# Five stages for all of a gated mixer's first product, with half of the modulation vector made in PE's column groups

## The chip, the cores and the metric

One Trainium2 chip, one of its cores. The metric is the device time of one execution in microseconds (us); a kernel's figure is the median of its runs. Before the change it is 2622.1 us (three runs, 2620.47 to 2630.4).

## What is computed

Three blocks on 256 rows of 2048 channels. The change lies in the first, and there in its entry:

```python
cond = silu(c)                               # one vector of 2048
mod = cond @ ada_w[i] + ada_b[i]             # 2048 x 6144
shift, scale, gate = split(mod, 3)
h = rms_norm(x, pre_g[i]) * (1 + scale) + shift
u, v, z = split(h @ w_in, 3)                 # 2048 x 12288
u = gelu(u); v = layer_norm(gelu(v), norm_g)
vm = einsum('gts,bnsgc->bntgc', w_s * mask, v) + b_s
y = (u * vm * silu(z)) @ w_out
x = x + gate * rms_norm(y, post_g[i])
```

All weights are float32 in HBM and are read once.

## The kernel before

Every weight matrix is loaded in chunks of 512 KB (two tiles of 128 rows by 512 columns) on SP's queue. A chunk ("piece") is split into a rounded part `wh` (ACT, line 239) and a remainder `wl` (DVE, line 242); PE multiplies three times for each tile of 128 rows (x high by wh, x high by wl, x low by wh: lines 301 to 303 with rows of x as stationary operand, 293 and 294 with weights as stationary operand). Six `raw` buffers hold loaded pieces, four pairs `wh`, `wl` hold split ones. `plan` writes the order of all loads into one list; `_issue` issues them in that order as buffers come free, `piece` hands split pieces to PE.

The first product is the v third of `h @ w_in`: eight groups of 512 columns, 16 tiles of 128 rows (k tiles) deep. It needs h, and h needs shift and scale of layer 0, that is 32 MB of `ada_w` before the last k tile. So the program goes in four stages of four k tiles each. `ada` loads scale and shift for the next 512 channels as eight chunks of 1 MB (rows of 512 columns) into a ring of five slots and multiplies them by `cond`: on DVE as one instruction for each 128 rows (lines 429 and 431), but for half of the scale's rows as a matmul with `cond` as a stationary operand of one column (line 427). Matmuls with ones (line 446) sum over the partitions and turn the row into a column, then `scale_done` and `h_tiles` (lines 569 to 574) make h. In each stage PE then takes v groups 3, 0, 1 and 2; groups 0 to 2 stay in six banks of PSUM over all stages, group 3 is summed in SBUF (lines 750 and 752, two banks). Groups 4 to 7 follow after the last stage as ordinary products (`gemm_tm`), and with them `spatial` loads and transposes `sgu_w_s` (lines 699 to 710), and `mix` puts 0.7 of a chunk of the remaining modulation (`rest`, 96 chunks of 512 KB: gate of layer 0, shift and scale of layer 1) beside each piece. Then come u (64 pieces) and z (64 pieces), with more of `rest`.

All engines work through their own instructions in the written order; waits are semaphores, so an instruction that waits holds up all behind it on its engine.

Of the kernel before, what the change touches and what calls it, by code (L numbers as in the profile page):

```python
# [16 lines left out]
P = 128  # L17
T = 256
# [53 lines left out]
class Kernel:  # L72
    def __init__(self, ctx, tc, ins, out):
# [4 lines left out]
        self.RAW, self.LOOK, self.AHEAD = 6, 3, 3  # L78
        self.g = ctx.enter_context(tc.tile_pool(name="g", bufs=1))
# [376 lines left out]
    def plan(self):  # L456
# [3 lines left out]
        self.h_done = [0] * 4  # L460
        for s in range(4):
            ring = [7, 8, 9, 10, 11]
            a = self.ada(0, 0, s, None, kt=4, ring=ring)
            b = self.ada(0, 1, s, (lambda s=s: self.h_stage(s)), kt=4, pe=2, ring=ring)
            if s == 0:
                for e in (b[0], a[0], b[1]):
                    e.ring = [1, 2, 3]
            E += [b[0], a[0], b[1], a[1], b[2], a[2], a[3], b[3]]
# [10 lines left out]
        for g in range(4, 8):  # L479
            main += self.group(("v", g), w_in, 4096 + g * 512, 16)  # L480
# [6 lines left out]
        E += self.mix(main, rest, [(40, 0.7), (64, 0.42), (64, 0.2), (56, 0.6)])  # L487
# [88 lines left out]
    def h_stage(self, s):  # L576
        self.scale_done(0, s)
        for j in range(4 * s, 4 * s + 4, 2):
            self.h_tiles(0, (j, j + 1), self.R0)
            self.split_ahead(2)  # L580


    def setup(self):
# [16 lines left out]
        nc.scalar.activation(out=self.cond, in_=ps[:, 0:16], func=AF.Silu)  # L600
        rows = self.slot(6).rearrange("p (a n) -> p a n", n=P)
# [8 lines left out]
        for tt in range(2):  # L610
            self._issue()
            nc.sync.dma_start(out=xt[tt], in_=i["x"][0, tt * P:tt * P + P, :])
        for _ in range(3):
            self._issue()
# [7 lines left out]
        self.wst = self.t("wst", [P, 16, P], pool=self.p0)  # L622
        self.bs = self.t("bs", [P, 16, P], pool=self.p0)
# [14 lines left out]
        self.prep_next()  # L638
        self.prep_next()
# [3 lines left out]
        for q in range(8):  # L643
# [6 lines left out]
            if q == 3:  # L650
                self.prep_next()
                self.prep_next()
# [8 lines left out]
        self.prep_next()  # L661
# [8 lines left out]
        self.start_stage()  # L670

    def start_stage(self):

        for _ in range(9):
            self.prep_next()

    def spatial(self, slot):
# [3 lines left out]
        ws = self.slot(slot).rearrange("p (g s) -> p g s", s=P)  # L681
        nc.sync.dma_start(out=ws, in_=i["sgu_w_s"][0].rearrange("g t s -> t g s"))
        nc.sync.dma_start(out=self.bs.rearrange("p g t -> p (g t)"), in_=i["sgu_b_s"].rearrange("o g t -> o (g t)").to_broadcast([P, 2048]))
        rows = self.slot(10)[:, 0:P]
        nc.vector.memset(rows[0:32, :], 0.0)
# [13 lines left out]
        nc.tensor.transpose(ps[:, 0:32], rows[0:32, :], self.identt[0:32, 0:32])  # L699
        yield  # L700
        nc.scalar.copy(self.cols[:, 2, 0:32], ps[:, 0:32])
        for q in range(4):
            ps = self.bank(5)
            for g in range(4):
                nc.tensor.transpose(ps[:, g * P:g * P + P], ws[:, q * 4 + g, :], self.identt)
# [7 lines left out]
    def sgu(self):  # L713
# [6 lines left out]
        def v_out(g):  # L720
            def evac(tt, ps):
                if uv[g] is None:
                    uv[g] = self.slot(4 + g).rearrange("p (i u t) -> p i u t", u=2, t=T)
                nc.scalar.activation(out=uv[g][:, :, 0, tt * P:tt * P + P], in_=ps.rearrange("p (i c) -> p i c", c=P), func=AF.Gelu, accum_out=stat[:, tt, g:g + 1])
            return evac

        banks = {(g, tt): self.bank(2 * g + tt) for g in range(3) for tt in range(2)}
        part = self.t("y4", [P, 4, T], pool=self.p0).rearrange("p (t i) n -> p t (i n)", t=2)
        self.banks([], [6])
        for s in range(4):  # L730
            self.split_ahead(2)
            for use in self.uses:
                if use:
                    use()
            self.uses = []
            for tt in range(2):
                banks[3, tt] = self.bank(6 + tt)
            for n in range(8):
                g = (3, 0, 1, 2)[n // 2]
                e, k0, kn, parts = self.piece(hold=s < 3)  # L740
                assert e.key == ("v", g)
                for tt in range(2):
                    ps = banks[g, tt]
                    for kk in range(kn):
                        k = n % 2 * 2 + kk
                        kt = s * 4 + k
                        self.mm_tm(ps, slice(0, 512), parts, kk, h(kt), tt, (k if g == 3 else kt) == 0, k == 3 if g == 3 else kt == 15)
                    if g == 3 and n % 2:
                        if s == 0:
                            nc.scalar.copy(part[:, tt, :], ps)  # L750
                        else:
                            nc.vector.tensor_tensor(out=part[:, tt, :], in0=part[:, tt, :], in1=ps, op=ALU.add)
                    if s == 3 and n % 2:
                        v_out(g)(tt, part[:, tt, :] if g == 3 else ps)
# [879 lines left out]
```

## Time and profile before

| | |
|---|---|
| median of three runs | 2622.1 us |
| the profiled execution | 2624.94 us, its span 2623.0 us |
| granted clock of TensorE, mean | 0.990 |
| busy PE, DVE, ACT | 98%, 71%, 53% of the span |
| read from HBM | 541.48 MB |

How to read it: PE is TensorE's matmul, PEld its load of the stationary operand, which runs beside PE. Busy time of PE is modelled, with overlapping records: the time that a matmul takes in a stream is the distance of starts. "Idle before" is how long the engine stood still before an instruction, with the releaser behind the arrow. Times within the program count from the start of the span. A float32 matmul that is not split leaves two records.

### The profile page before, as it was taken

What the parts mean: (1) busy time and instruction counts of PE and PEld (TensorE: products, weight loads), DVE (VectorE), ACT (ScalarE), POOL (GpSimd) and SP (SyncE); (2) the same over time, 40 slices, a digit from 0 to 9 for tenths busy, and PEclk for the clock granted to TensorE, in tenths of its full rate; (3) what the DMA queues carried; (4) which work ended last, traced back from release to release, by engine and by line L of the source; (5) the groups of instructions that cost most, each with busy time, mean ns of one, the idle gap of its engine ahead of it and who ended that gap; (6) DMA issues with size and microseconds to landing.
All of it is one profiled execution on the core that took longest, in us unless ns stands there. A gap on an engine that the chain in (4) does not pass through costs nothing. (4 is left out here: it accounts for less than half of the span.)

```text
span 2623.0 us, 36858 instructions
## 1 busy us (share of the span) xinstructions
PE 2558.0 (98%) x13884; PEld 2169.7 (83%) x13884; DVE 1852.5 (71%) x2700; ACT 1385.1 (53%) x2101; POOL 0.2 (0%) x4
## 2 busy tenths in 40 slices
PE   7999999999998999998999999999999999999999
PEld 4577888888886888887888888888888888888887
DVE  6877877777776778766778677668665555666665
ACT  3243644545454655556556666555544545555554
POOL 0000000000000000000000000000000000000000
PEclk8999999999998999999999999999999999999999
DMA  9989888666884677644545444555556666565664
GB/s 365 353 278 313 275 273 263 209 210 215 293 273 152 182 227 220 204 157 153 159 137 170 152 149 150 193 193 193 193 178 192 187 191 187 185 198 192 192 194 128
DMA packets 298524, 546.00 MB, mean 208 GB/s; under 512 B 27370, under 2 KB 40426, under 8 KB 297962
## 3 DMA queue, kind: packets, MB, share of 16 engines
q1 hardware_dynamic: 296618, 542.71, 64.2%
q8 instruction: 108, 1.77, 0.3%
q10 hardware_dynamic: 1728, 0.94, 0.1%
q14 instruction: 70, 0.57, 0.1%
HBM read 541.48 MB, written 2.10 MB: 207 GB/s over the span
## 5 line engine op out<-in xcount | busy, mean ns | idle before, releaser
L293 PE MATMUL b<-s,wh 128*128 128x512 f32 x4800 | 1696.8, 397 | 5.9 <-DVE s L941 4.6
L239 ACT CAST wh<-raw 128x1024 fp32r<-128x1024 f32 (+2 forms) x840 | 866.2, 1039 | 984.0 <-PE b L293 615.1
L294 PE MATMUL b<-s,wl 128*128 128x256 f32 x4800 | 1345.6, 280 | 0.5 <-DVE wl L242 0.5
L242 DVE TENSOR_TENSOR wl<-raw,wh 128x1024 fp32r<-128x1024 f32 (+2 forms) x840 | 1002.8, 1211 | 298.8 <-ACT wh L239 294.4
L293 PEld LDWEIGHTS b<-s,wh 128*128 128x128 f32 x4800 | 905.7, 189 | 208.4 <-issue 8.1
L294 PEld LDWEIGHTS b<-s,wl 128*128 128x128 f32 x4800 | 905.8, 189 | 1.6 <-DVE wl L242 0.8
L301 PE MATMUL b<-wh,s 128*128 128x512 f32 x816 | 329.3, 403 | 7.1 <-ACT s L570 6.1
L303 PE MATMUL b<-wh,s 128*128 128x512 f32 x816 | 323.7, 397 | 0.0
L302 PE MATMUL b<-wl,s 128*128 128x512 f32 x816 | 322.2, 395 | 1.3 <-DVE wl L242 1.3
L301 PEld LDWEIGHTS b<-wh,s 128*128 128x128 f32 x816 | 154.4, 189 | 51.2 <-ACT s L570 6.4
L314 DVE TENSOR_TENSOR cb<-b,ca 128x256 f32<-128x256 f32 x258 | 108.5, 422 | 115.0 <-ACT ca L308 110.9
L369 DVE TENSOR_TENSOR s<-s,s 128x1024 fp32r<-128x1024 f32 (+1 forms) x82 | 91.6, 1121 | 135.9 <-ACT s L368 135.9
L303 PEld LDWEIGHTS b<-wh,s 128*128 128x128 f32 x816 | 154.1, 189 | 39.6 <-DVE s L574 0.4
L302 PEld LDWEIGHTS b<-wl,s 128*128 128x128 f32 x816 | 154.5, 189 | 38.1 <-DVE wl L242 2.1
L431 DVE SCALAR_TENSOR_TENSOR ada<-raw,cond,ada 128x512 f32<-128x512 f32 x240 | 179.5, 748 | 3.5
L308 ACT COPY ca<-b 128x256 f32<-128x256 f32 x338 | 122.7, 366 | 45.5 <-PE b L294 34.1
L368 ACT CAST s<-s 128x1024 fp32r<-128x1024 f32 (+1 forms) x82 | 78.8, 961 | 12.7 <-DVE s L1010 6.6
L431 DVE SCALAR_TENSOR_TENSOR ada<-s,cond,ada 128x512 f32<-128x512 f32 x88 | 65.4, 751 | 7.8 <-DMA s<-in_ada_w 5.4
L314 DVE TENSOR_TENSOR s<-b,ca 128x256 f32<-128x256 f32 x72 | 29.9, 420 | 24.6 <-ACT ca L308 24.4
L293 PE MATMUL b<-yat,wh 128*128 128x512 f32 x128 | 44.4, 392 | 0.0
L427 PE MATMUL b<-s,cond 128*1 128x512 f32 x64 | 34.1, 660 | 8.4 <-DMA s<-in_ada_w 8.4
L1582 ACT ACTIVATE s<-s 128x256 f32<-128x256 f32 x64 | 26.8, 419 | 17.3 <-DVE s L1581 15.1
(305 smaller groups left out, 1451.5 us busy)
## 6 DMA issues: line engine op xcount, KB each, us to landing
raw<-in_sgu_w_in SPq DMA_DIRECT2D x192, 512.0 KB
raw<-in_w_in SPq DMA_DIRECT2D x148, 512.0 KB
raw<-in_ada_w SPq DMA_DIRECT2D x128, 512.0 KB
raw<-in_w_up SPq DMA_DIRECT2D x128, 512.0 KB
raw<-in_w_down SPq DMA_DIRECT2D x128, 512.0 KB
s<-in_ada_w SPq DMA_DIRECT2D x32, 1024.0 KB
raw<-in_sgu_w_out SPq DMA_DIRECT2D x64, 512.0 KB
raw<-in_mla_w_in SPq DMA_DIRECT2D x40, 512.0 KB
```

The costliest lines, as they stand in the source:

```text
L239: self.nc.scalar.copy(h, v[:, k0:k0 + kn, :])
L242: self.nc.vector.tensor_tensor(out=l, in0=v[:, k0:k0 + kn, :], in1=h.bitcast(F32), op=ALU.subtract)
L293: mm(ps[:, 0:512], h[:, kk, wsl], x, start=start, stop=False, skip_group_check=True)
L294: mm(ps[:, 0:256], l[:, kk, wsl], x[:, 0:256], start=False, stop=stop, skip_group_check=True)
L301: mm(ps, x[:, a:a + P], h[:, kk, wsl], start=start, stop=False, skip_group_check=True)
L302: mm(ps, x[:, a:a + P], l[:, kk, wsl], start=False, stop=False, skip_group_check=True)
L303: mm(ps, x[:, 256 + a:256 + a + P], h[:, kk, wsl], start=False, stop=stop, skip_group_check=True)
L308: self.nc.scalar.copy(c, ps[:, 256:512])
L314: self.nc.vector.tensor_tensor(out=o, in0=ps[:, 0:256], in1=c, op=ALU.add)
L368: self.nc.scalar.copy(dst[:, :, 0:256], raw)
L369: self.nc.vector.tensor_tensor(out=dst[:, :, 256:512], in0=raw, in1=dst[:, :, 0:256].bitcast(F32), op=ALU.subtract)
L431: nc.vector.scalar_tensor_tensor(out=acc[0], in0=v[:, k - k0, :], scalar=col, in1=acc[0], op0=ALU.mult, op1=ALU.add)
```

## The change

All eight v groups are now made in the stages, of which there are five, with 2, 2, 4, 4 and 4 k tiles. Groups 6 and 7 stay in four banks of PSUM; the other six share three banks in turn and are summed in SBUF after each stage (line 945, ACT copies, in the first; line 947, DVE adds, in the others), in the slots that later hold u and v, in `y4` and in `wst`. The whole of the scale goes to PE as float32 matmuls with a stationary operand of 32 columns (`condz`: `cond` in column 0, the rest zeros), each k tile of four in another group of 32 columns of the array (line 891, `tile_position`); an ACT copy (line 897) takes the four rows back. The whole of the shift goes to DVE (lines 875 and 877). Loads for the first two stages have rows of 256 columns, eight k tiles to a chunk. `walk` is the one list of pieces, modulation chunks and finishing steps from which all engines' instructions are written. `spatial` moves into u, and `rest` is mixed 0.75 to a piece of u and 0.24 to a piece of z, where it was 0.7 (v groups 4 to 7 and part of u), 0.42 and 0.2.

```diff
+        self.STAGES, self.ORDER, self.STAY = [0, 2, 4, 8, 12, 16], (0, 1, 6, 2, 3, 7, 4, 5), (6, 7)
...
-            a = self.ada(0, 0, s, None, kt=4, ring=ring)
-            b = self.ada(0, 1, s, (lambda s=s: self.h_stage(s)), kt=4, pe=2, ring=ring)
...
-            for g in (3, 0, 1, 2):
-                for k in range(2):
-                    E.append(self.chunk(("v", g), w_in, s * 512 + k * 256, 4096 + g * 512))
+            k0, k1 = self.STAGES[s + 1:s + 3]
+            n = (k1 - k0) * P
+            kt = 2048 // n
+            for r in range(0, 16, kt):
+                for part in range(2):
+                    e = self.chunk(None, i["ada_w"][0], r * P, part * 2048 + k0 * P, kt, n)
...
+            room = max(1, len(pieces) - 3)
...
+            put("rows", s=s + 1)
+            for kind, e, at in pieces[room:room + 1]:
+                put(kind, e, **at)
+            put("fin", s=s + 1)
+            for kind, e, at in pieces[room + 1:]:
+                put(kind, e, **at)
...
-        for g in range(4, 8):
-            main += self.group(("v", g), w_in, 4096 + g * 512, 16)
...
-        E += self.mix(main, rest, [(40, 0.7), (64, 0.42), (64, 0.2), (56, 0.6)])
+        E += self.mix(main, rest, [(64, 0.75), (64, 0.24), (56, 0.6)])
...
+        def mod(at):
...
+                q = slice(k % 4 * 32, k % 4 * 32 + 32)
+                nc.tensor.matmul(st["rows"][q, 0:n], self.condz[:, kt, :], v[:, k, :], start=kt < 4, stop=kt >= 12, tile_position=(0, k % 4 * 32), skip_group_check=True)
...
+        def product(at):
...
+                    if stay:
+                        b = self.STAY.index(g) * 2 + tt
+                    else:
+                        b = 4 + st["turn"] % 3
+                        st["turn"] += 1
...
+                if not stay:
+                    to = parts[g, tt]
+                    if s == 0:
+                        nc.scalar.copy(to, four(ps))
+                    else:
+                        nc.vector.tensor_tensor(out=to, in0=to, in1=four(ps), op=ALU.add)
...
+            if kind == "w" or kind == "mod":
+                ahead(4 if kind == "w" else 3)
```

How the order moves at three places. In the names `raw` is a loaded piece, `wh` and `wl` its two parts, `ada` a modulation sum, `b4` to `b6` the shared banks, `s7` to `s11` the ring of modulation chunks; the last number is a serial number.

DVE in the second stage before: one sum outside PSUM for the stage, behind the third split.

```order
L574 SCALAR_TENSOR_TENSOR s1_56_237<-cb_120_509,mod0_7_74,s1_56_237 128x256
L574 SCALAR_TENSOR_TENSOR s1_56_237<-cb_121_512,mod0_7_74,s1_56_237 128x256
L242 TENSOR_TENSOR wl_125_521<-raw_101_385,wh_112_480 128x1024
L242 TENSOR_TENSOR wl_131_533<-raw_105_409,wh_124_519 128x1024
L242 TENSOR_TENSOR wl_133_549<-raw_106_411,wh_130_531 128x1024
L752 TENSOR_TENSOR y4_67_248<-y4_67_248,b6_122_517 128x512
L752 TENSOR_TENSOR y4_67_248<-y4_67_248,b7_123_518 128x512
L242 TENSOR_TENSOR wl_135_567<-raw_107_413,wh_132_547 128x1024
L429 TENSOR_SCALAR ada_137_584<-s10_110_451,cond_8_75 128x512
```

DVE in the second stage now, from the split of the stage's first piece to the first sum.

```order
L859 TENSOR_TENSOR wl_114_464<-raw_78_291,wh_113_462 128x1024
L875 TENSOR_SCALAR ada_115_466<-s10_67_252,cond_8_75 128x512
L877 SCALAR_TENSOR_TENSOR ada_115_466<-s10_67_252,cond_8_75,ada_115_466 128x512 x3
L859 TENSOR_TENSOR wl_119_477<-raw_81_297,wh_118_475 128x1024
L877 SCALAR_TENSOR_TENSOR ada_115_466<-s7_82_307,cond_8_75,ada_115_466 128x512 x4
L859 TENSOR_TENSOR wl_125_505<-raw_87_329,wh_124_503 128x1024
L877 SCALAR_TENSOR_TENSOR ada_115_466<-s9_105_426,cond_8_75,ada_115_466 128x512 x4
L859 TENSOR_TENSOR wl_132_535<-raw_94_362,wh_131_533 128x1024
L947 TENSOR_TENSOR s4_51_195<-s4_51_195,b4_134_539 128x4x128
L947 TENSOR_TENSOR s4_51_195<-s4_51_195,b5_135_547 128x4x128
```

Between the first split and the first sum stand three further splits and three chunks of shift; the sum of bank b4_134 comes behind all of them.

PE at the same place now: the scale's four matmuls, and the second piece's product.

```order
L891 MATMUL b7_136_555<-s11_75_285,bs_11_82 32x512 x4
L303 MATMUL b6_142_574<-wh_118_475,s0_45_189 128x512
L304 MATMUL b6_142_574<-wl_119_477,s0_45_189 128x512
L305 MATMUL b6_142_574<-wh_118_475,s0_45_189 128x512
L303 MATMUL b6_142_574<-wh_118_475,s0_45_189 128x512
L304 MATMUL b6_142_574<-wl_119_477,s0_45_189 128x512
L305 MATMUL b6_142_574<-wh_118_475,s0_45_189 128x512
L303 MATMUL b4_143_582<-wh_118_475,s0_45_189 128x512
L304 MATMUL b4_143_582<-wl_119_477,s0_45_189 128x512
```

The second half of this piece goes into b4_143, which is the bank of b4_134.

DVE at the change to the third stage now, behind the first sums over partitions.

```order
L605 SCALAR_TENSOR_TENSOR s1_46_190<-cb_162_696,mod0_7_74,s1_46_190 128x256
L605 SCALAR_TENSOR_TENSOR s1_46_190<-cb_163_699,mod0_7_74,s1_46_190 128x256
L859 TENSOR_TENSOR wl_165_706<-raw_128_515,wh_164_704 128x1024
L600 SCALAR_TENSOR_TENSOR cb_167_710<-x_13_87,a10_26_117,R_42_181 128x256
L600 SCALAR_TENSOR_TENSOR cb_168_713<-x_13_87,a10_26_117,R_42_181 128x256
L605 SCALAR_TENSOR_TENSOR s1_46_190<-cb_167_710,mod0_7_74,s1_46_190 128x256
L605 SCALAR_TENSOR_TENSOR s1_46_190<-cb_168_713,mod0_7_74,s1_46_190 128x256
L875 TENSOR_SCALAR ada_169_718<-s8_137_560,cond_8_75 128x512
L877 SCALAR_TENSOR_TENSOR ada_169_718<-s8_137_560,cond_8_75,ada_169_718 128x512 x3
L859 TENSOR_TENSOR wl_171_725<-raw_133_537,wh_170_723 128x1024
L947 TENSOR_TENSOR wst_55_199<-wst_55_199,b6_174_731 128x512
L947 TENSOR_TENSOR wst_55_199<-wst_55_199,b4_175_739 128x512
```

The sum of bank b6_174, the bank that the last piece of the stage before (b6_180) takes for its second half, stands behind four instructions of h, a chunk of shift and two splits.

## Rows read from the trace of the kernel before

**Rows 1.** The page, part 1 (busy us) and the granted clock of part 2.
```profile
PE 2558.0 (98%) x13884; PEld 2169.7 (83%) x13884; DVE 1852.5 (71%) x2700; ACT 1385.1 (53%) x2101; POOL 0.2 (0%) x4
...
PEclk8999999999998999999999999999999999999999
```

**Rows 2.** Windows: busy us and (instructions) of PE, PEld, DVE, ACT, POOL; clock; DMA share; GB/s.
```profile
40.00:75.80 35.80, 33.74 (x129) 21.65 (x129) 31.04 (x46) 11.64 (x16) 0.00 (x0) 0.95 1.02 370
...
149.00:266.90 117.90, 114.94 (x507) 92.19 (x507) 84.87 (x95) 54.94 (x77) 0.00 (x0) 1.00 0.89 300
266.90:449.80 182.90, 182.90 (x1068) 161.42 (x1067) 135.44 (x180) 103.13 (x166) 0.00 (x0) 1.00 0.82 268
```

**Rows 3.** Timeline 0 to 48 us: start, duration, engine, line, idle before and releaser.
```profile
9.57 1.91 ACT L641 ACTIVATE x<-s 128x2048 f32<-128x2048 f32 x1 [5.87 <-DMA s<-in_x]
...
31.96 3.57 PE L427 MATMUL b<-s,cond 128*1 128x512 f32 x4 [4.73 <-DMA s<-in_ada_w]
...
35.46 3.57 PE L446 MATMUL b<-ones,ada 128*128 128x1 f32 x16
...
39.07 0.16 DVE L448 TENSOR_TENSOR mod<-b,cols 128x4 f32<-128x4 f32 x1 [1.55 <-PE b L446]
...
40.55 0.80 PE L301 MATMUL b<-wh,s 128*128 128x512 f32 x1 [1.51 <-ACT s L570]
```

**Rows 4.** Timeline of PE, 44 to 76 us.
```profile
44.10 0.40 PE L301 MATMUL b<-wh,s 128*128 128x512 f32 x1
...
46.20 0.40 PE L301 MATMUL b<-wh,s 128*128 128x512 f32 x1
...
50.49 1.88 PE L427 MATMUL b<-s,cond 128*1 128x512 f32 x4
...
72.32 1.95 PE L446 MATMUL b<-ones,ada 128*128 128x1 f32 x16
```

**Rows 5.** Groups of DVE by form, 40 to 76 us: count, busy us, mean ns, idle before.
```profile
L431 DVE SCALAR_TENSOR_TENSOR ada<-s,cond,ada 128x512 f32<-128x512 f32 x22 | 16.3, 751 | 1.0 <-DMA s<-in_ada_w 0.4
L242 DVE TENSOR_TENSOR wl<-raw,wh 128x1024 fp32r<-128x1024 f32 x8 | 9.5, 1217 | 0.4 <-ACT wh L239 0.4
...
L569 DVE SCALAR_TENSOR_TENSOR cb<-x,a,R 128x256 f32<-128x256 f32 x5 | 2.2, 481 | 0.0
L429 DVE TENSOR_SCALAR ada<-s,cond 128x512 f32<-128x512 f32 x2 | 1.0, 479 | 0.0
```

**Rows 6.** The same, 76 to 112 us: the sum outside PSUM.
```profile
L752 DVE TENSOR_TENSOR y<-y,b 128x512 f32<-128x512 f32 x2 | 1.4, 686 | 0.1
```

**Rows 7.** DMA, 90 to 98 us: packets, MB, share of 16 engines.
```profile
q1 hardware_dynamic: 1573, 3.09, 105.1%
```

**Rows 8.** DMA, 1276 to 1284 us, rows of 2 KB, queue not full.
```profile
q1 hardware_dynamic: 1054, 2.04, 77.7%
```

**Rows 9.** DMA, 1244 to 1252 us, nearly all rows of 1 KB, queue not full.
```profile
DMA packets 1083, 1.10 MB, mean 137 GB/s; under 512 B 33, under 2 KB 1059, under 8 KB 1083
...
q1 hardware_dynamic: 1083, 1.10, 48.6%
```

**Rows 10.** Instructions of line 427: ns min/median/max, first and last start.
```profile
L427 PE MATMUL b<-s,cond x64: 590/592/1061, 7.2 to 142.1; 128*1 128x512 f32 x64
```

**Rows 11.** Instructions of line 301, 200 to 300 us.
```profile
L301 PE MATMUL b<-wh,s x85: 392/392/501, 200.1 to 266.4; 128*128 128x512 f32 x85
```

**Rows 12.** Timeline of PE, 195 to 262 us: two of its waits.
```profile
216.96 0.50 PE L301 MATMUL b<-wh,s 128*128 128x512 f32 x1 [1.06 <-ACT wh L239]
...
225.17 0.66 PE L705 MATMUL b<-ident,s 128*128 128x128 f32 x4 [1.13 <-ACT cols L701]
```

**Rows 13.** Groups of DVE by form, 266.9 to 449.8 us (u).
```profile
L242 DVE TENSOR_TENSOR wl<-raw,wh 128x1024 fp32r<-128x1024 f32 x64 | 77.8, 1222 | 24.6 <-ACT wh L239 23.6
L431 DVE SCALAR_TENSOR_TENSOR ada<-raw,cond,ada 128x512 f32<-128x512 f32 x54 | 40.4, 748 | 0.7
L314 DVE TENSOR_TENSOR cb<-b,ca 128x256 f32<-128x256 f32 x32 | 13.2, 422 | 15.6 <-ACT ca L308 15.2
```

More of the change, by code (lines that the diff above doesn't have):

```diff
@@ new lines, in put @@
+        def put(kind, e=None, **at):
+            if e:
+                at["n"] = len(E)
+                E.append(e)
+            self.walk.append((kind, at))
+        for s in range(-1, len(self.STAGES) - 1):
+            pieces = []
+            if s >= 0:
+                k0, k1 = self.STAGES[s:s + 2]
+                for g in self.ORDER:
+                    for k in range(k0, k1, 2):
+                        pieces.append(("w", self.chunk(("v", g), w_in, k * P, 4096 + g * 512), dict(s=s, g=g, k=k)))
+            if s + 2 == len(self.STAGES):
+                for kind, e, at in pieces:
+                    put(kind, e, **at)
+                break
+            k0, k1 = self.STAGES[s + 1:s + 3]
+            n = (k1 - k0) * P
+            kt = 2048 // n
+            mods = []
+            for r in range(0, 16, kt):
+                for part in range(2):
+                    e = self.chunk(None, i["ada_w"][0], r * P, part * 2048 + k0 * P, kt, n)
+                    e.kind, e.ring = "ada0", [7, 8, 9, 10, 11]
+                    mods.append(("mod", e, dict(s=s + 1, part=part, r=r, kt=kt)))
+            done = 0
+            room = max(1, len(pieces) - 3)
+            for q in range(room if pieces else 0):
+                put(*pieces[q][:2], **pieces[q][2])
+                while done < len(mods) and (done + 0.5) * room < (q + 1) * len(mods):
+                    put(*mods[done][:2], **mods[done][2])
+                    done += 1
+            for kind, e, at in mods[done:]:
+                put(kind, e, **at)
+            put("rows", s=s + 1)
+            for kind, e, at in pieces[room:room + 1]:
+                put(kind, e, **at)
+            put("fin", s=s + 1)
+            for kind, e, at in pieces[room + 1:]:
+                put(kind, e, **at)
@@ L610, in setup @@
         for tt in range(2):
-            self._issue()
             nc.sync.dma_start(out=xt[tt], in_=i["x"][0, tt * P:tt * P + P, :])
-        for _ in range(3):
+        for _ in range(2):
             self._issue()
@@ L669, in setup, with spatial @@
         columns(1)
[L670 to L677, printed above, removed]
+    def spatial(self):
         nc, i = self.nc, self.i
         yield from self.idle(40)
[L681 to L682 removed]
+        self.wst = self.t("wst", [P, 16, P], pool=self.p0)
+        self.bs = self.t("bs", [P, 16, P], pool=self.p0)
+        nc.sync.dma_start(out=self.wst, in_=i["sgu_w_s"][0].rearrange("g t s -> t g s"))
         nc.sync.dma_start(out=self.bs.rearrange("p g t -> p (g t)"), in_=i["sgu_b_s"].rearrange("o g t -> o (g t)").to_broadcast([P, 2048]))
[L684 to L685 removed]
+        rows = self.t("rows", [32, P], pool=self.p0)
+        nc.vector.memset(rows, 0.0)
         rp = lambda ap: ap.rearrange("(b p) -> b p", p=P)
@@ L698, in spatial @@
         ps = self.bank(5)
[L699 removed]
+        nc.tensor.transpose(ps[:, 0:32], rows, self.identt[0:32, 0:32])
         yield
@@ L723, in evac @@
                     uv[g] = self.slot(4 + g).rearrange("p (i u t) -> p i u t", u=2, t=T)
-                nc.scalar.activation(out=uv[g][:, :, 0, tt * P:tt * P + P], in_=ps.rearrange("p (i c) -> p i c", c=P), func=AF.Gelu, accum_out=stat[:, tt, g:g + 1])
+                nc.scalar.activation(out=uv[g][:, :, 0, tt * P:tt * P + P], in_=ps, func=AF.Gelu, accum_out=stat[:, tt, g:g + 1])
             return evac
[L727 to L754, printed above, removed]
-                if n < 7 and s < 3:
-                    self.prep_next()
-            if s < 3:
-                self.start_stage()
-        self.banks([0, 1, 2, 3, 4, 7], [6])
-        self.lanes[0].append(self.spatial(11))
-        for g in range(4, 7):
-            self.gemm_tm(("v", g), 16, h, v_out(g))
-        self.drain(0)
-        self.gemm_tm(("v", 7), 16, h, v_out(7))
+        self.stages(h, uv, v_out)
+        self.banks([0, 1, 2, 3, 4, 7], [6])
+        self.lanes[1].append(self.spatial())
         def normalise():
```

145 lines of the change are left out of this document (123 added, 22 removed).

## The prediction

> **What bounds the kernel now.** Read the page first: PE is busy 98% of the span at nearly the full clock [rows 1], so what counts is work on PE and the time before PE has work. The windows by stage show where PE is below that: at the start and in the stages [rows 2]. There the first product begins only at 40.55 us, 8.6 us after PE got the last chunk of scale at 31.96 [rows 3], and the first stage takes 35.2 us (40.55 to its successor at 75.78, 1.5 us of it waiting for h), though its 96 matmuls at 0.233 us (nine of them from 44.10 to 46.20) are 22.4 us [rows 4]. DVE is busy 31 to 33 us of such a stage and DMA runs at 370 GB/s [rows 2]: three resources are nearly full there. After the stages PE is dense: the last v group ends at 267.0 (last start on line 301 at 266.4, two more matmuls behind it) [rows 11], u ends at 449.8. From there nothing changes in kind, so I work out when v ends and what u then costs.
>
> All times are made against the profiled execution, 2624.94 us; the median of the runs shown is 2622.1, so 2.8 us come off at the end. A measurement of this kernel can tell about 0.5% from no change, 13 us.
>
> **PE's own work.** The product keeps its 768 matmuls of v: 768 x 0.233 = 179.2 us. The one-column matmuls go: each stage had eight in four visits of 1.88 us [rows 4], 7.5 us, three stages of them after the product began. In their place come 14 visits after the product begins: two of eight matmuls of 256 columns, twelve of four of 512.
>
> The price of such a visit is the unknown on which most hangs. A float32 matmul of 512 columns takes 0.94 us (two in 1.88) and leaves two records: 64 records for 32 matmuls [rows 4, 10]. Lower bound: all four abreast in one matmul's time, with a tenth more for the change of layout, 1.05 us. Upper bound: one behind the other, 4 x 0.94 = 3.76 us. I take a value between: the two passes of one matmul use the same 32 columns, so the second waits for the first, and since PE starts in order, the next matmul can start only beside that second pass. Four then take five passes of 0.47 us, 2.35 us; eight of 256 columns take nine of 0.235, 2.1 us. Sum: 2 x 2.1 + 12 x 2.35 = 32.4 us, where before it was 22.6. By the lower bound it would be 14.7, by the upper 52.6.
>
> The Trainium skill, page "TensorE: Matmul & The Clock Gate", section "Part 3: Packing small matmuls", lets matmuls in different column groups run side by side, 2.38 times as fast for three; this is the first rival below, and no row here shows it. Its page "TensorEngine Tiling (Array Packing)", section "Key Properties", says that a change of tiling mode drains the array, which would happen twice in each visit; it gives no price.
>
> Sums over partitions: 16 records in 1.95 us [rows 4]; four later finishes give 0.5 + 3 x 1.0 = 3.5 us.
>
> **The start.** Before, 2 MB of x and 8 MB of modulation land before PE's last chunk; now 2 and 4. A full queue moves 387 GB/s, 2.71 us for a chunk of 1 MB [rows 7]. But the chunks of the first two stages have rows of 1 KB. Packets cost 16 x 8 us x share / count: for 1 KB rows 57.4 ns, for 2 KB rows 94.4 ns, both with the queue not full [rows 8, 9]. A chunk of the same size then costs between 2.71 us (no loss) and 3.7 us (0.61 of the time for half the bytes, and no gain from a full queue); I take 3.3. x is in by some 9.5 us (its first half was needed at 9.57 [rows 3], with a chunk before it). Four chunks and 0.4 us of small loads later it is 23.1 us. Then eight matmuls (2.1), a copy of the rows (0.6), the sum (0.5 at the full 2.4 GHz: before, the 16 records took 3.57 us behind an idle 4.73 us, half the clock, and 1.95 later; here PE idles some 1.5 us) [rows 3, 4], and 2.0 for mod and h (39.07 to 40.55, and a bit of waiting [rows 3]): the first product starts at 28.3 us, 12.2 earlier. With chunks of 2.71 us it is 26.
>
> **DVE's work.** The shift is all DVE's, 2 x (16 x 0.48) + 3 x (0.48 + 15 x 0.75) = 50.6 us [rows 5], where it had 24 instructions for each of four stages. New are 48 sums outside PSUM at 0.69 us [rows 6], 33 us. With 64 splits of 1.22 us and 32 instructions of 0.48 us for h, DVE has some 180 us of work while v lasts: it is not full. What costs is its order.
>
> **New waits in the stages.** A shared bank is free only after its sum. In the second stage the first sum stands behind four splits and three chunks of shift, and the third chunk is the 21st MB of the queue: 9.5 + 0.4 + 8 x 3.3 + 11 x 2.71 = 66.1 us. Behind it come 4 x 0.75 + 1.22 + 0.69, so bank b4 is free at 71; PE, at the second half of the second piece, is there at 67 and waits **4 us**, all that follows with it. At the change to the third stage the sum of b6 stands behind mod, eight instructions for h, two splits and a chunk: 0.5 + 3.8 + 2.4 + 2.7 + 0.7 = 10.2 us after the finish, while PE has 1.5 pieces, 4.2 us, to do: a wait of **6 us**. At the next change it is one split more against two pieces and a half, 11.4 against 7.0: **4.4 us**. At the last no chunk is left: **1.7 us**. In the first stage PE waits 3 us for the second split (0.9 us of h, eight of shift at 0.48 and the split stand before it), and 2 us for ACT's copies out of b5 and b6, which stand behind casts that wait for loads; one more us in the third. Together 22.2 us. Going are the four waits of 1.5 us for h and half-clock stretches.
>
> **Sum for v.** 28.3 + 179.2 + 32.4 + 3.5 + 22.2 = 265.6 us, where v ended at 267.0: a gain of 1.4 us. The earlier start is given back, most of it to visits (10) and waits.
>
> **What u takes over.** Two finishes of `rest` (2.0 us), 17 transposes of `spatial` at 0.165 (2.8) with their wait (1.1) and waits for loads held up by its 2 MB (1.8 in sum before, one of them 1.06) [rows 4, 12]: 7.7 us. These stood inside the 267.0 before. u was PE's without a gap [rows 2], so they lie on the path. The chunks of `rest` themselves are DVE's: 19 more in u, 38 instructions, 28 us, on 135.4 busy [rows 2, 13]; with 15.6 us of waiting for ACT's copies it is 179 of 190, so they hide, barely. z keeps its load within two chunks.
>
> Total: -1.4 + 7.7 = +6.3 us. 2624.9 + 6.3 = 2631.2, and on the median **2628 us**, no change that can be told.
>
> **Rivals.**
>
> *Abreast and ahead.* Visits cost 1.05 us: 17.7 us less, of which 4 fall into waits for loads and DVE, so 14 less. And if loads come as fast as rows of 2 KB and DVE catches up before the bank is asked for, half of the 22 us of waits goes as well: 2628 - 14 - 11 = 2603. For it: DVE and DMA each have slack over the whole of v. Against it: the written order of the sums, which no slack moves. With the visits alone, 2614.
>
> *No concurrency.* Each visit is 3.76 us, in sum 20 more, and 1.7 at the start: 2628 + 22 = 2650, slower than before. It decides from about 2.8 us for a visit of four. For it: in the trace every float32 pass stands alone, 0.47 us behind the one before, and nothing shows two at once [rows 10]. Against it: the four write different rows of the bank and share no column of the array. Drains at each change of layout push the same way.
>
> *DVE becomes the bound of u.* If its waits grow with its load, or the 16 instructions of the layer norm fall on the dense stretch, PE waits for `wl`: the margin of 11 us is gone and u is 7 us longer, 2635.
>
> That the change does not do what it says is small: the order shows the visits, sums and stages where the words of the change put them.
>
> **How the numbers follow.** Forecast 0.40 (2615 to 2640), abreast and ahead 0.32, no concurrency 0.17, u bound by DVE 0.11. Faster than 2609: 0.27, from the first rival alone (its rest, 0.05, lies within 0.5%). Slower than 2635: 0.17 from no concurrency, 0.06 of the u case and 0.08 of the forecast's upper end, 0.31. Same: 0.42. The range takes both ends of the visit's price and of the loads: 2602 to 2652.
>
> **What would show it.** Right: the first product near 28 us; visits on line 891 of some 2.3 us from first to last start plus a pass; PE waits for line 947 at the second piece of the second stage and at the end of each stage, 4 to 6 us; v ending near 266; u about 8 us longer. Wrong: visits of 1 us, no wait for sums, v ending before 250 (faster); visits of 3.8 us and v ending near 288 (slower); u with waits of PE for `wl` (DVE the bound).

## The result and the profile after

The changed kernel takes 2649.06 us (median of four runs, 2648.47 to 2654.35); the kernel before, on the same chip, 2624.14 us (four runs). The ratio is 1.0095 with a 95% interval of 1.0074 to 1.0116: slower, by 25 us. The forecast was 2628 us and no change that can be told; the range of 2602 to 2652 holds the result near its end. The profiled execution after took 2649.23 us, its span 2647.4 us, the mean granted clock is 0.985.

The page, part 1 and the granted clock of part 2, of the changed kernel, against [rows 1]:

```profile
PE 2560.2 (97%) x13980; PEld 2177.9 (82%) x13980; DVE 1855.4 (70%) x2726; ACT 1393.6 (53%) x2116; POOL 0.7 (0%) x5
...
PEclk8899999999999999999999999999999999999999
```

Busy sums hardly move; the span grew by 24.4 us, so look by stage. The windows of the changed kernel, against [rows 2]: five stretches of v, then u.

```profile
28.20:62.00 33.80, 31.71 (x148) 23.02 (x148) 24.30 (x39) 17.57 (x26) 0.00 (x0) 0.93 1.06 377
62.00:107.00 45.00, 33.07 (x147) 22.87 (x147) 33.85 (x49) 11.54 (x15) 0.00 (x0) 0.85 1.01 370
107.00:170.00 63.00, 54.76 (x241) 39.38 (x240) 41.99 (x55) 18.77 (x21) 0.00 (x0) 0.94 0.74 254
170.00:226.00 56.00, 51.67 (x234) 37.60 (x233) 37.49 (x49) 18.78 (x21) 0.00 (x0) 0.97 0.55 185
226.00:271.20 45.20, 44.93 (x187) 36.33 (x188) 25.87 (x28) 26.37 (x45) 0.00 (x0) 0.96 0.62 188
271.20:467.90 196.70, 190.88 (x1092) 166.92 (x1091) 162.93 (x223) 104.89 (x172) 0.00 (x0) 0.97 0.90 313
```

From 62 to 107 us PE is busy for 33 of 45 us, at 0.85 of the clock, and DVE for 33.85: neither engine is full, they wait for each other. In u PE had no gap before; now it stands 5.8 us of 196.7, and the clock is 0.97.

Where the span grew, by instructions that end a stage (last start of the product in v, last copies of u and z, first and last result of the third block's up product), in us:

| kernel | v ends | u | z | z to up | up | behind it |
|---|---|---|---|---|---|---|
| before | 266.4 | 183.0 | 194.4 | 1280.5 | 337.5 | 361.2 |
| changed | 270.5 | 197.3 | 195.9 | 1281.8 | 340.7 | 361.2 |
| difference | +4.1 | +14.3 | +1.5 | +1.3 | +3.2 | 0 |

So v ends 4 us later although it starts 12.3 us earlier, u is 14 us longer, and 6 us are lost in stages whose instructions the change leaves alone (z gets about one chunk of `rest` more).

The visits, in the timeline of PE of the changed kernel (start, duration, engine, line, idle before and releaser; compare [rows 4]):

```profile
61.80 0.40 PE L305 MATMUL b<-wh,s 128*128 128x512 f32 x1
62.12 1.06 PE L891 MATMUL b<-s,bs 128*32 128x512 f32 x8
63.12 0.50 PE L303 MATMUL b<-wh,s 128*128 128x512 f32 x1
```

Four float32 matmuls of 512 columns, eight records, are done in 1.06 us, where two took 1.88 before. The next product matmul starts 1.00 us after the visit began, and the visit 0.32 after the last product matmul in place of 0.233. The forecast's 2.35 us is refuted and its lower bound, 1.05, is right. The sum of the 14 visits is 16.0 us with these edges, not 32.4.

The start, in the timeline of PE of the changed kernel: the last chunk of scale and the sums over partitions.

```profile
22.28 1.93 PE L891 MATMUL b<-s,bs 128*32 128x256 f32 x16 [3.58 <-DMA s<-in_ada_w]
24.71 1.86 PE L909 MATMUL b<-ones,ada 128*128 128x1 f32 x8 [0.49 <-ACT ada L897]
```

The chunk is there 0.8 us earlier than forecast; the sum takes 1.86 us, not 0.5.

And one of the waits, in the same timeline, at the change to the third stage:

```profile
94.10 0.40 PE L305 MATMUL b<-wh,s 128*128 128x512 f32 x1
100.66 0.80 PE L303 MATMUL b<-wh,s 128*128 128x512 f32 x1 [6.16 <-DVE wst L947]
101.25 0.63 PE L304 MATMUL b<-wl,s 128*128 128x512 f32 x1
101.68 0.63 PE L305 MATMUL b<-wh,s 128*128 128x512 f32 x1
...
103.81 0.63 PE L304 MATMUL b<-wl,s 128*128 128x512 f32 x1
104.24 0.58 PE L305 MATMUL b<-wh,s 128*128 128x512 f32 x1
104.66 0.39 PE L303 MATMUL b<-wh,s 128*128 128x512 f32 x1
104.88 0.39 PE L304 MATMUL b<-wl,s 128*128 128x512 f32 x1
```

PE waits 6.16 us for a sum, as forecast (6), but the nine matmuls behind the wait start 0.43 apart, not 0.233: PE runs at 1.2 GHz until 104.6. This wait is paid twice. What DVE does in that wait (its timeline, changed kernel):

```profile
90.63 0.88 DVE L600 SCALAR_TENSOR_TENSOR cb<-x,a,R 128x256 f32<-128x256 f32 x2
...
96.03 0.48 DVE L875 TENSOR_SCALAR ada<-s,cond 128x512 f32<-128x512 f32 x1
96.55 2.33 DVE L877 SCALAR_TENSOR_TENSOR ada<-s,cond,ada 128x512 f32<-128x512 f32 x3
98.79 1.22 DVE L859 TENSOR_TENSOR wl<-raw,wh 128x1024 fp32r<-128x1024 f32 x1
99.92 1.28 DVE L947 TENSOR_TENSOR wst<-wst,b 128x512 f32<-128x512 f32 x2
```

The sum that frees the bank stands behind eight instructions of h, a chunk of the next stage's shift and two splits, in the written order. PE's waits from 28 to 271 us, by releaser (the view of waits, changed kernel: total, times, longest):

```profile
PE b L303 <- DVE wst L947: 13.0, 3, 6.2
PE b L303 <- DVE s L947: 11.8, 5, 5.8
PE b L303 <- ACT s L601: 1.7, 1, 1.7
PE b L304 <- DVE wl L859: 1.5, 2, 0.9
PE b L303 <- ACT s L945: 0.6, 1, 0.6
```

24.8 us of it are eight waits for line 947, for a shared bank; the 1.7 us for line 601 stand before the first product matmul and are part of the start. Distances of starts of all PE instructions between the first product matmul and the end of v, sorted by what they are, give both sides of the sum (us; rows of the timeline, 767 product matmuls at 0.237 in the mean; a matmul counts as half clock when its record is longer than 0.55 us, and v ends here with the last matmul's own 0.4 us):

| term | forecast | changed | before |
|---|---|---|---|
| first product matmul | 28.3 | 28.2 | 40.5 |
| product at full clock | 179.2 | 181.8 | 181.8 |
| visits of the modulation | 32.4 | 16.0 | 22.8 |
| sums over partitions | 3.5 | 5.9 | 7.5 |
| waits | 22.2 | 26.8 | 8.0 |
| half clock: 49 matmuls (before 21), 0.21 more each | 0 | 10.2 | 4.3 |
| starting anew behind waits | 0 | 1.7 | 0.6 |
| transposes | in u | in u | 1.7 |
| v ends | 265.6 | 270.9 | 266.8 |

The columns add up to within 1 us.

### The profile page after: what moved, and what is told of

Its sections match the earlier page's. It is cut to its first block, busy times and chain, and to the rows that moved or that the text cites. A ratio compares the mean times of both kernels' runs of the same rounds, so it can differ in the third digit from the quotient of the medians.

```text
span 2647.4 us, 37110 instructions
## 1 busy us (share of the span) xinstructions
PE 2560.2 (97%) x13980; PEld 2177.9 (82%) x13980; DVE 1855.4 (70%) x2726; ACT 1393.6 (53%) x2116; POOL 0.7 (0%) x5
## 5 line engine op out<-in xcount | busy, mean ns | idle before, releaser
L241 ACT CAST wh<-raw 128x1024 fp32r<-128x1024 f32 (+2 forms) x776 | 801.2, 1040 | 894.5 <-PE b L295 578.8
L244 DVE TENSOR_TENSOR wl<-raw,wh 128x1024 fp32r<-128x1024 f32 (+2 forms) x776 | 925.0, 1210 | 263.9 <-ACT wh L241 261.0
L303 PEld LDWEIGHTS b<-wh,s 128*128 128x128 f32 x816 | 155.9, 191 | 79.8 <-DVE wst L947 14.3
L857 ACT CAST wh<-raw 128x1024 fp32r<-128x1024 f32 x64 | 66.2, 1046 | 102.8 <-PE b L305 57.5
L859 DVE TENSOR_TENSOR wl<-raw,wh 128x1024 fp32r<-128x1024 f32 x64 | 77.7, 1223 | 45.6 <-ACT wh L857 45.5
L370 ACT CAST s<-s 128x1024 fp32r<-128x1024 f32 (+1 forms) x82 | 78.8, 962 | 12.7 <-DVE s L1134 6.5
L877 DVE SCALAR_TENSOR_TENSOR ada<-s,cond,ada 128x512 f32<-128x512 f32 (+1 forms) x75 | 48.3, 645 | 8.9 <-DMA s<-in_ada_w 6.5
```

The source lines that it names most:

```text
L241: self.nc.scalar.copy(h, v[:, k0:k0 + kn, :])
L244: self.nc.vector.tensor_tensor(out=l, in0=v[:, k0:k0 + kn, :], in1=h.bitcast(F32), op=ALU.subtract)
L303: mm(ps, x[:, a:a + P], h[:, kk, wsl], start=start, stop=False, skip_group_check=True)
L370: self.nc.scalar.copy(dst[:, :, 0:256], raw)
```

## The experiments

Each kernel is the changed one with the edit shown. Ratios are to the kernel before, timed in the same session; its median was 2624.14 to 2628.58 us over the sessions, so a difference of medians between sessions is good to some 4 us only. The theory after reading the traces was: the early start and the cheap visits are worth about 19 us in v, and the three shared banks give it all back, once as waits and once as half clock behind them; u stalls because of `spatial`; and stages that nobody edited pay for where buffers now lie in SBUF.

**1. Where the buffers lie.** The eight slots of SBUF that are not yet in use are claimed at the start, in the order in which the kernel before comes to them, which is to give them and the `raw` buffers the addresses that they had there.

```diff
         xt = [self.slot(4), self.slot(5)]
+        for k in (1, 2, 3, 7, 8, 9, 10, 11):
+            self.slot(k)
```

> Only addresses differ from the changed kernel: the slots of the global pool are claimed at the start in the order of the kernel before, so h, the raw buffers and the ring lie where they lay there. Theory (in the last block's up product PE runs 1% slower after the change, 395 against 392 ns a matmul, because its operand moved in SBUF): the time from 1946 us to the last square of that block falls from 340.7 us back to some 337.4, and the whole from 2649 to 2645 or a little less. Rival (it varies from run to run): the up product stays at 340 to 341 us, the whole at 2649.

Measured: 2641.94 us, ratio to before 1.0056 [1.0036, 1.0076], 7 us less than the changed kernel. v and u do not move (271.3, 196.6); z takes 195.0, z to up 1278.9 and up 337.4, 7.1 us less in sum. The up product shows it best: groups of PE over that stage, first of the changed kernel, then of this one.

```profile
L295 PE MATMUL b<-s,wh 128*128 128x512 f32 x962 | 337.4, 394 | 0.0
```

```profile
L295 PE MATMUL b<-s,wh 128*128 128x512 f32 x963 | 334.6, 392 | 0.0
```

No wait in either, and full clock: the same matmuls run 1% slower when only addresses differ. The other traces bear it out: in all six with the slots claimed (this run and runs 8 to 12) up takes 337.4 to 337.5 us and z to up 1276.1 to 1279.2, in all seven without 340.7 and 1281.0 to 1287.3. That addresses do it is shown for up; by what mechanism was not tried.

**2. Five shared banks for three.** Only column group 7 stays in PSUM; group 6 joins those summed in SBUF (its sums lie in the free columns of `bs`), and two banks come free for the turn.

```diff
-        self.STAGES, self.ORDER, self.STAY = [0, 2, 4, 8, 12, 16], (0, 1, 6, 2, 3, 7, 4, 5), (6, 7)
+        self.STAGES, self.ORDER, self.STAY = [0, 2, 4, 8, 12, 16], (0, 1, 6, 2, 3, 7, 4, 5), (7,)
...
+            parts[6, tt] = four(self.room[:, 512 + tt * 512:1024 + tt * 512])
...
-                        b = 4 + st["turn"] % 3
+                        b = 2 + st["turn"] % 5
```

> One edit to the changed kernel: five shared banks in place of three, only group 7 stays, group 6 is summed in SBUF too (8 more sums of 0.69 us on DVE, 2 more copies on ACT). Theory (PE waits for the sum of a shared bank, then runs on at half clock): the waits of PE for line 947, 24.8 us in the changed kernel, fall below 8, the granted clock of 62 to 107 us rises from 0.85 above 0.95, v ends near 240 us where it ended at 271, and the whole is near 2618. Rival (DVE or the loads bound the stages, the bank is only where it shows): other waits take the place, v ends after 260 and the whole stays above 2638.

Measured: 2627.13 us, ratio 1.0006 [0.9995, 1.0018]: 22 us less than the changed kernel, though DVE has eight sums more. v ends at 247.1, 23.4 us earlier. Its waits in v (28 to 248 us; the sum stands in line 949 of this kernel):

```profile
PE b L303 <- DVE s L949: 4.1, 2, 3.8
PE b L303 <- DVE wst L949: 3.4, 1, 3.4
PE b L304 <- DVE wl L861: 3.0, 3, 1.2
PE b L303 <- ACT s L601: 1.7, 1, 1.7
```

Waits for sums fall from 24.8 to 7.5 us, matmuls at half clock from 49 to 22 (5.4 us less); that is the 23 us. What the change lost in v hung on the number of banks in turn, not on DVE's load. The gain was still smaller than expected: v ends at 247 and not 240, and the clock from 62 to 107 us is 0.89, not above 0.95, as two waits of 3.4 and 3.8 us stay. The profiled execution, 2631.35 us, is one of its longer ones: z to up took 1287.0 us in it, 5 more than in the changed kernel. The stalls there are the same, but more stretches behind them ran at half clock, as at 1040.6 to 1065.6 us; the ten executions of this kernel lie between 2624.88 us (mean clock 0.989) and this one (0.986). That such stretches make the difference between executions is likely but not shown, since each kernel has one trace.

**3. `spatial`'s loads spread over u.** Pauses of 12 and 4 steps between its loads on SP.

```diff
         nc.sync.dma_start(out=self.wst, ...)
+        yield from self.idle(12)
...
```

> One edit to the changed kernel: the eleven loads of the spatial weights and small rows are spread over some 60 steps of u instead of standing together on SP's queue. Theory (the 13.8 us without a load of a piece, 302 to 316 us, empty the raw buffers; PE idles 5.8 us and runs on at half clock): PE's waits in u vanish, u falls from 196.6 us to 186, the whole from 2649 to 2639. Rival (the 19 added chunks of modulation make DVE or DMA the bound of u): u stays above 192.

Measured: 2647.22 us, ratio 1.0075 [1.005, 1.0099]; u takes 198.0 us, no less. The wait of 4.3 us for `wh` is gone, but PE now waits 3.2 us for `cb` and 2.1 us for `cols`, ahead of the transposes of `spatial`, and falls to half clock behind that. The expected gain did not come, and the rival's sign, u above 192, did. One load shows what the spreading did to SP: `bs` straight behind `wst` in the changed kernel, and 9.6 us after it here.

```profile
303.70 5.90 SPq L697 DMA_DIRECT2D bs<-in_sgu_b_s  x1
```

```profile
313.49 0.42 SPq L698 DMA_DIRECT2D bs<-in_sgu_b_s  x1
```

So SP's longest time between two loads of weights, start to start, falls from 13.8 to 6.1 us, and u is as long as before the edit: the lateness was handed on.

**4. The same visits one behind the other.** All sixteen k tiles of the scale go into column group 0; the copy and the sum take 32 rows.

```diff
-                q = slice(k % 4 * 32, k % 4 * 32 + 32)
+                q = slice(0, 32)
...
-    ... start=kt < 4, stop=kt >= 12, tile_position=(0, k % 4 * 32), ...
+    ... start=kt == 0, stop=kt == 15, tile_position=(0, 0), ...
...
```

> One edit to the changed kernel: all matmuls of the scale use the same 32 columns of the array, so they can't stand abreast; only those 32 rows are copied and summed. Theory (four abreast cost 1.06 us where one behind the other cost 3.8, and PE's time is on the path): a visit takes 3.8 us, v ends 20 to 35 us later, the whole is near 2675. Rival (the visits fall into waits that are there anyway): visits take 3.8 us, v ends less than 12 us later, the whole is below 2662. Third (array layout doesn't matter, the passes overlap in one column group too): a visit stays below 2 us.

Measured: 2683.37 us, ratio 1.0213 [1.0191, 1.0235], 34 us more than the changed kernel. The timeline of PE of this kernel, against 1.06 us above:

```profile
67.24 3.62 PE L891 MATMUL b<-s,bs 128*32 128x512 f32 x8
70.79 0.50 PE L303 MATMUL b<-wh,s 128*128 128x512 f32 x1
```

The same four matmuls take 3.62 us, 3.4 times as long. So they do run abreast, and it is worth the 29 us by which v ends earlier with it. (In run 4 u is 5.8 us longer too, at 203.1; why was not tried.) The Trainium skill, page "TensorE: Matmul & The Clock Gate", section "Part 3: Packing small matmuls — row/col tiling", gives 2.38 times for three column tiles; the trace agrees in kind, with 3.4 times for four in float32. The price that I put in its place (each matmul's second pass waiting for its first, with only the next matmul beside it) is not borne out. The page "TensorEngine Tiling (Array Packing)", section "Key Properties", says that a change of mode drains the array: the rows show some 0.1 us on either side of a visit, alike in the kernel before, where `cond` alone is the stationary operand, so no price of such a drain can be told from them.

**5. Zeros that keep PE awake.** Sixteen matmuls with zero weights between the two halves of three pieces, where the waits of 5.77, 6.16 and 4.52 us stood; they add zeros to the half just finished.

```diff
+                if tt == 0 and (s, g, k) in self.FILL:
+                    for _ in range(self.FILL[s, g, k]):
+                        nc.tensor.matmul(ps[0:31, :], self.condz[:, 0, 1:32], self.x[:, 0:2, :], start=False, stop=False, skip_group_check=True)
```

> Sixteen matmuls with zero weights (they add zeros to a finished or running half, so the result is whole) stand between the two halves of three pieces, where TensorE waited 5.77, 6.16 and 4.52 us for a bank at 64.8, 94.5 and 162.5 us. Theory (each long wait is paid twice: as the wait, and as half clock behind it, 7 + 9 + 13 matmuls at 0.43 in place of 0.233 us): the waits end when they did, the matmuls behind them start 0.233 apart, v ends about 6 us earlier (264.5 in place of 270.5), the time is about 2643 us. Rival (VectorE's lateness is the bound of these stages, and half clock only fills what would be waited for anyway): the next waits for the sums grow by as much, v ends at 270 and the time is 2649 us; if the zeros hold up the sum of their half, 2652 or more.

Measured: 2648.35 us, ratio 1.0081 [1.0067, 1.0095], the same as without. PE at the place shown above, in this kernel's timeline:

```profile
93.74 4.46 PE L942 MATMUL b<-x,bs 128*31 128x512 f32 x10
99.09 0.51 PE L304 MATMUL b<-wh,s 128*128 128x512 f32 x1 [0.89 <-DVE wst L951]
99.43 0.40 PE L305 MATMUL b<-wl,s 128*128 128x512 f32 x1
```

The matmuls behind the wait keep their 0.233 us, and 25 in place of 49 in v ran at half clock. That half of the theory is shown. But the sixteen took 14.3 us where the waits shrank by 12.2, the visits cost 1.4 more, and v ends only 1.4 us earlier (269.1). The 24 matmuls that ran at full clock instead are worth 24 x 0.21 = 5.0 us: half clock behind waits is a real cost in v, but zeros of a fixed number are not the way to have it back.

**6. Four stages of four k tiles.**

```diff
-        self.STAGES, self.ORDER, self.STAY = [0, 2, 4, 8, 12, 16], (0, 1, 6, 2, 3, 7, 4, 5), (6, 7)
+        self.STAGES, self.ORDER, self.STAY = [0, 4, 8, 12, 16], (0, 1, 6, 2, 3, 7, 4, 5), (6, 7)
```

> Four stages of four k tiles, as before the change, all else as changed. Theory (the early start is given back in the two short stages): the first product starts some 8.6 us later, at 36.8 us (four more chunks of 1 MB at 2.71 less nothing else), but the second stage's waits for banks (5.77 and one of the two long waits at changes) go with the half clock behind them and one finish, together 12 to 14 us: v ends near 266, time 2643 to 2646 us. Rival (an early start is worth itself): v ends near 279, time 2657 us.

Measured: 2650.2 us (2644.13 to 2653.85), ratio 1.0087 [1.007, 1.0105]. The product starts at 40.9 us, later than I expected, as three visits wait for their chunks (1.1, 4.4 and 4.8 us), and v still ends at 266.5, 4 us before that of five stages. So in v the start 12.7 us earlier is given back in the short stages, as the theory has it. In total nothing is gained, since in the profiled execution z to up took 1287.3 us, with the same half-clock stretches as in run 2. The rival's 279 for v is out.

**7. Less of `rest` in u.** 13 chunks of 1 MB move from u to z.

```diff
-        E += self.mix(main, rest, [(64, 0.75), (64, 0.24), (56, 0.6)])
+        E += self.mix(main, rest, [(64, 0.55), (64, 0.44), (56, 0.6)])
```

> The chunks of rest are spread otherwise: 0.55 for each piece of u in place of 0.75, 0.44 for each of z in place of 0.24 (13 chunks of 1 MB move from u to z). Theory (u lengthened because DMA, 0.92 busy there against 0.82 before, cannot bring its weights in time behind spatial's 2 MB; the wait of 4.3 us and the half clock behind it follow): the wait for wh at 317 us falls to about 1 us, u takes 189 us in place of 197, z 1 us more, time about 2642 us. Rival (the gap of 13.8 us in which SP issues spatial's loads makes the wait, whatever else is loaded): u stays at 197 and the time at 2649 us.

Measured: 2643.48 us, ratio 1.0066 [1.0053, 1.008], 5.6 us less. u takes 190.9 us, z 196.6. Half clock in u goes entirely and PE waits 3.6 us in place of 5.8; one wait of 3.2 us (now for `cb`) stays. DMA's share is part of u's loss, not all.

**8. The three together** (slots, five banks, the mix of run 7).

> Three edits together: the allocation order of the slots (7 us less alone), five shared banks in place of three with only the last column group kept in PSUM (22 us less alone), and the chunks of rest spread as in the run beside it (7 us less if that theory holds). Theory (they cost at different places, so the gains add): 2649 - 7 - 22 - 7 = 2613 us, 0.995 of the kernel before. Rival (the chunks moved to z or the slots give nothing beside the banks): 2620 to 2627 us, the same as before.

Measured: 2614.75 us (five runs), ratio 0.9957 [0.9944, 0.9971]: the gains add, and the kernel is faster than the one before. v ends at 247.4, u takes 191.2, z to up 1276.8, up 337.4.

**9 to 12. What is left in u.** Run 8 still has one stall, 3.15 us at 298 us. SP's own timeline in that kernel shows what goes on ahead of it:

```profile
276.39 0.37 SPq L173 DMA_DIRECT2D raw<-in_sgu_w_in  x1
276.97 0.86 SPq L699 DMA_DIRECT2D wst<-in_sgu_w_s  x1
277.93 4.66 SPq L700 DMA_DIRECT2D bs<-in_sgu_b_s  x1
...
289.00 0.37 SPq L713 DMA_DIRECT2D blk<-in_shape_consts  x1
289.47 0.40 SPq L173 DMA_DIRECT2D raw<-in_ada_w  x1
```

For 12.7 us SP issues no weights. From about 287 to 290 us the DMA engines have almost nothing to move (their busy share in the same kernel, 276 to 292 us, 0.4 us to a digit), and ACT waits 9.56 us for a piece:

```profile
DMA  5599889879899999999999999862100000059579
```

```profile
294.83 1.05 ACT L241 CAST wh<-raw 128x1024 fp32r<-128x1024 f32 x1 [9.56 <-DMA raw<-in_sgu_w_in]
```

So in the last 3 us of that the weights are late for want of an issue, not of bandwidth. PE's wait ends at 298.05 us with `cb`, which needs ACT's copy out of the bank, and that copy stands behind the late piece in ACT's order. Four edits of run 8: `spatial` starts 120 steps into u instead of 40; still less of `rest` in u; `spatial`'s loads on ScalarE's queue; the same on GpSimd's.

```diff
-        yield from self.idle(40)
+        yield from self.idle(120)
```

> The three edits as before, and spatial's loads start 120 steps of its lane into u in place of 40. Theory (the stall at 298 us, 3.15 us and half clock behind it, comes from 2 MB and 11 issues of spatial falling together with ScalarE's first copies of u, 14 to 15 of 20 us busy there against 9 to 10 later): the stall goes, u takes 186 us in place of 191, time 2610 us. Rival (SP's 12 us of issues stall the weights wherever they stand): the same stall some 50 us later, time 2615 us.

```diff
-        E += self.mix(main, rest, [(64, 0.55), (64, 0.44), (56, 0.6)])
+        E += self.mix(main, rest, [(64, 0.45), (64, 0.54), (56, 0.6)])
```

> The three edits as before, with 0.45 chunks of rest for each piece of u and 0.54 for each of z. Theory of DMA (u's stall shrinks as rest leaves it: 197 to 191 us with 13 chunks fewer): with six or seven chunks fewer again u takes 188 us, z half a us more, time 2612 us. Rival (what the first 13 chunks did not take away is SP's gap, which no mix moves): u stays at 191 us, time 2615 us.

```diff
-        nc.sync.dma_start(out=self.wst, ...)
+        nc.scalar.dma_start(out=self.wst, ...)
...
```

> The three edits as before, and spatial's 11 loads (2 MB) issued on ScalarE's queue in place of SP's. Theory (u's stall comes from SP, which issues no weights for 12 us while it issues these 11 loads, 4.7 to 5.9 us of it for bs alone): SP goes on, but ScalarE, which rounds the weights, is held for the same 12 us: the stall stays about 3 us and the time about 2614 us; if the issues cost ScalarE little, u takes 187 us and the time is 2611 us. Rival (2 MB more in a full queue make the stall, whoever issues them): u stays at 191 us, 2615 us, with the weights landing late.

```diff
-        nc.sync.dma_start(out=self.wst, ...)
+        nc.gpsimd.dma_start(out=self.wst, ...)
...
```

> The same on GpSimd's queue; GpSimd has nothing else to do in this stage. Theory (SP's gap): SP issues weights without a gap from 277 to 289 us, the stall of 3.15 us and the half clock behind it go, u takes 187 us, time 2611 us. Rival (bandwidth): the stall of about 3 us stays, u 191 us, time 2615 us.

| run | us | ratio to before | u | longest wait of PE in u |
|---|---|---|---|---|
| 8, as it is | 2614.75 | 0.9957 [0.9944, 0.9971] | 191.2 | 3.1, `cb` |
| 9, later | 2612.05 | 0.9944 [0.9927, 0.996] | 191.8 | 3.7, `cols` |
| 10, less rest | 2615.16 | 0.9953 [0.9938, 0.9968] | 192.1 | 6.0, `cb` |
| 11, ScalarE's queue | 2616.81 | 0.9973 [0.996, 0.9986] | 195.9 | 6.7, `wh` |
| 12, GpSimd's queue | 2606.91 | 0.9936 [0.992, 0.9953] | 185.8 | none |

Runs 9 and 10 speak for their rivals: neither a later place nor still fewer bytes takes the stall away. On ScalarE, which rounds the weights, the issues do more harm than on SP. On GpSimd, which has nothing else to do, the stall is gone; v's end and u by windows in run 12 (GpSimd busy for 6.9 us):

```profile
28.00:247.40 219.40, 209.24 (x951) 154.79 (x952) 166.08 (x226) 92.90 (x129) 0.00 (x0) 0.97 0.85 293
247.40:433.00 185.60, 185.57 (x1085) 163.38 (x1084) 147.62 (x198) 105.20 (x172) 6.88 (x12) 1.00 0.88 295
```

and the two large loads in the timeline of GpSimd:

```profile
249.68 1.33 POOL L699 DMA_DIRECT2D wst<-in_sgu_w_s  x1 [248.43 <-ACT s L741]
251.00 0.56 POOL L700 DMA_DIRECT2D bs<-in_sgu_b_s  x1
```

u is as dense as before the change, with as many bytes as in run 8. They leave 27 us earlier too, since GpSimd had no weights to issue ahead of them; SP's gap and this earlier start go together in this run and are not told apart. This has the lowest time of the study, 0.6% below the kernel before; the intervals of runs 8 to 10 overlap with its own, but its trace ends 6 us before that of run 8, with no wait of PE in u.

## Why the prediction was right and wrong

- **The start** is right in sum, 28.2 us for 28.3, by two errors that cancel: the chunk came 0.8 us earlier, and the sum over partitions, priced "at the full 2.4 GHz" with 0.5 us, took 1.86.
- **The price of a visit** is wrong: "the second waits for the first, and since PE starts in order, the next matmul can start only beside that second pass", 2.35 us. Measured 1.06; run 4 shows what no concurrency would be, 3.62. This step alone would have made the forecast 16 us too slow.
- **The sums over partitions** were misread: a later finish leaves 16 records, as in [rows 4], so by its 1.95 us three of them and a half come to 6.8 us, not 3.5; measured 5.9. The product itself took 2.6 us more than 0.233 us a matmul.
- **The new waits** are right in cause, and at the four main places in size too: forecast 4, 6, 4.4 and 1.7 us, measured 5.77, 6.16, 4.52 and 2.31. The sum, 26.8 for 22.2, also has errors that cancel: the 5 us of the first stage were 2.1, and waits of 1.83 to 1.89 us for sums in the third and fourth stage, three in number, had 1 us in the forecast. "The written order of the sums, which no slack moves" held against the first rival: the cheap visits gave DVE nothing. But the order was only half of it; two banks more (run 2) took most of these waits away.
- **The clock** is the term that was left out. I counted the "half-clock stretches" of before as going, and none as coming. In v the clock costs 10.2 us where it cost 4.3, and starting anew behind waits 1.7.
- **u**: forecast 7.7 us more, measured 14.3. The finishes (1.6 for 2.0) and the transposes (1.6 for 2.8) are no dearer than forecast; waits are 5.8 for 2.9, with 5.1 us of half clock and new starts behind them (product matmuls of u 184.5 us by distances of starts, 179.4 before), which is the same omission. DVE was busy 162.9 us in u, and yet is not its bound: PE waited for rounded weights that had been issued late, and with `spatial`'s loads on another queue, and earlier, the wait is gone (run 12). The reason given, "loads held up by its 2 MB", was wrong in part: the bytes are moved in run 12 too. How much is due to the issue, how much to the bytes (run 7) and how much to the time stays open, as run 3 cut SP's gap from 13.8 to 6.1 us and gained nothing.
- **What no term had**: 6 us in z and behind it. "From there nothing changes in kind" missed that the edit moves buffers; run 1 gives 7.1 us back.
- **The rivals.** *No concurrency* gave 2650, a time that came true while its mechanism, by run 4, is false. *Abreast and ahead* had the visits right and the waits wrong. The errors of the forecast have both signs: 16 us too much for visits; too little by 5 for waits, 12 for the clock and new starts in v, 5 for the product and the sums, 7 for u and 6 for the stages behind it. So "no change that can be told" was wrong, by 18 us on the profiled executions, and that the range held is luck in part.

## What to carry to other kernels

When a change lets PE wait, cost each wait of several microseconds at its length and add the half clock behind it (here 16.5 us in the three longest waits, and 29 matmuls at half clock and the new starts behind them, some 7 us), and ask first how many banks stand between PE and the engine that frees them: two banks more were worth 22 us, while DVE's work grew. Ask what a queue cannot issue while it issues something else: here eleven loads kept SP from the weights for 12.7 us, and with them on the queue of an engine that nobody waits for, and earlier, PE's wait was gone. And when untouched stages change, compare addresses before looking for a cause in the schedule.

## What the runs showed of the hardware

- Four float32 matmuls with 32 columns of weights, each in its own column group, take 1.06 us (512 columns each), one group for all four 3.62 us.
- The same stream of matmuls (the up product, some 960 pairs in each trace), with no wait and at the full granted clock, takes 340.7 or 337.4 us depending on where buffers lie in SBUF.
- A load that copies 8 KB to each of 128 partitions (`bs`) holds SP for 3.94 to 5.90 us when it is issued straight behind the 1 MB of `wst`, for 0.42 us when 9.6 us lie between them (run 3); GpSimd it holds for 0.56 us straight behind `wst` (run 12). The Trainium skill, page "DMA: Bandwidth & Descriptors", section "Issuing engine by pattern", names SyncE for simple loads and calls its path generally faster; here the move of eleven loads to GpSimd's queue took the wait of 3.1 us and 5 us of u away, and the measurement decides.
- Behind waits of 5.77, 6.16 and 4.52 us in v PE started at 1.2 GHz and was back at 2.4 after 3.1, 4.0 and 5.7 us. Behind the wait of 2.31 us it started at 2.4, fell 1.3 us later and was back after 3.4 us. In u, with waits of 4.32, 0.47 and 1.04 us close together, it was at 1.2 from 321.3 to 329.9 us.
